# Half-row products of a recurrence, tied behind the first product of each of their two banks

## The chip, the cores and the metric

The kernel runs on one core of one Trainium2 chip, in float32. The metric is the device time of one execution in microseconds (us); lower is better. Engines by the profile's names: PE is TensorE (PEld its weight loads), DVE VectorE, ACT ScalarE, POOL GpSimd, SP SyncE, which issues the transfers.

## The reference

One layer of a hybrid block over 256 latent and 256 context tokens of width 2048. A modulated norm feeds one input projection (10,304 columns in all). Its columns go to a bidirectional RWKV-7 recurrence of 16 heads of 64 (the "time mixing"), to a latent attention of 8 heads, and to gates; the branches are merged, projected and added to the input.

What matters here is the recurrence and what prepares it:

```python
def rwkv_prepare(u_rkv, u_wd, u_ad, conv_w, w0, w_decay_up, a0, w_a_up, k_k, k_a):
    B, L, _ = u_rkv.shape
    r, k, v = jnp.split(centred_short_conv(u_rkv, conv_w), 3, axis=-1)
    wd = jnp.tanh(u_wd.reshape(B, L, 2, DECAY_LORA))
    w_log = (w0 + jnp.einsum("bldr,drc->bldc", wd, w_decay_up)).astype(f32)
    decay = jnp.exp(-jnp.exp(-jax.nn.softplus(-w_log) - 0.5))
    a = jax.nn.sigmoid((a0 + jnp.einsum("bldr,drc->bldc",
                                        u_ad.reshape(B, L, 2, AAA_LORA), w_a_up)).astype(f32))
    ...

def rwkv7_step(S, xs):
    r, w, k, v, kk, akk = xs
    sa = jnp.einsum("dbhij,dbhj->dbhi", S, -kk)
    S = S * w[..., None, :] + sa[..., :, None] * akk[..., None, :] + v[..., :, None] * k[..., None, :]
    return S, jnp.einsum("dbhij,dbhj->dbhi", S, r)
```

The two einsums with `w_decay_up` and `w_a_up` are low-rank products of rank 64, one for each of the two directions d. The scan runs over the context tokens first and then over the latent ones, forwards and backwards.

## The kernel before

The program is written for a framework that orders the instructions of each engine at compile time by priority: program order, unless a block raises its priority by a number of places. Each engine then works its own queue in that order and waits on semaphores. Tiles come from pools; a tile of a pool's tag takes one of its buffers when a former holder has been read for the last time.

The recurrence handles two heads (a pair p) at a time on 128 partitions, 64 for each, in chunks of 64 tokens. Each pair has two halves, `h // 2` = p and `h % 2` = 0 for context, 1 for latent tokens: 16 halves in all, in nine groups. `front` (line 691) prepares a half, `front2` (line 836) transposes its values and keys, `diagonal` (line 869) inverts 16x16 blocks by way of DRAM, and `back` (line 913) computes inverses of the chunks (products into PSUM tag `lv`) and steps through the chunks (tag `ch`, tiles `chp`, products with `UV`, `xs`, `M`). The function `drive` (line 545) writes the order of all this in program order, from an estimate of TensorE's time that each product adds (`Tensor.add`), and puts steps of a background between them: projections with the big weights (`proj_g`, line 410, tile `acc`) in bursts.

A burst (`Tensor.burst`, line 99) leaves its first product, the head, at its own priority, and gives all that follow in the block a priority raised by `HB` = 600 places and a dependency on the head without a semaphore (`BEHIND`), so that they come soon behind it in TensorE's queue. Before the change only the projections use it (and, later, `branch_g`).

Two places in `front` have products that read 64 of the 128 rows and write one of two banks each:

- `lr` (line 712): the low-rank products. The directions d lie on the two halves of the rows (`hss`), and direction d writes bank `lr[d]`. For each of two column halves j there are three products (high and low parts in fp32r) per direction: twelve in all, 64 rows, 256 columns. Both banks come from tag `wk`, which has two buffers. In a context half `unit_keys` (line 668) runs ahead and has its own tiles there; the last, transposes of `rnb`, is read by the instruction that makes `kk` (line 688). ScalarE reads both `lr` banks with two activations each (`th`, and the sums in `En`).
- `pv` (line 787), latent halves alone, twice each (`cp`): sixteen products of keys with queries (tiles `BK` and `QR`), 64 rows, 128 columns, head g of the pair on half g of the rows into bank `pv[g]`. VectorE masks them into `AQ` and `AR`.

Of the kernel before, what the change touches and what calls it, by code (L numbers as in the profile page):

```python
# [19 lines left out]
T = 256  # L20
# [34 lines left out]
BEHIND = mybir.DependencyInfo(mybir.DependencyClass.NoSync, mybir.DependencyReason.DATA)  # L55
# [29 lines left out]
class Tensor:  # L85
# [10 lines left out]
    head = None  # L96

    @contextmanager
    def burst(self, tc):

        self.tc, self.head = tc, ()
        yield
        self.head = None

    def matmul(self, out, lhsT, rhs, **kw):
        n, k, m = math.prod(rhs.shape[1:]), lhsT.shape[0], math.prod(lhsT.shape[1:])
        if lhsT.dtype == F32R:
            self.add((max(256, n) / 2400 + 0.003) * k / 128, n * k / 128)
        elif m <= 64:
            self.add(n / 1200 + 0.044, 2 * n * k / 128)  # L110
        else:
            self.add((max(512, 4 * n) / 2400 + 0.005) * max(k, 64) / 128, 2 * n * k / 128)
        if not self.head:
            i = self.engine.matmul(out, lhsT=lhsT, rhs=rhs, **kw)  # L114
            if self.head == ():
                self.head = i
            return i
        with self.tc.high_priority(HB):
            i = self.engine.matmul(out, lhsT=lhsT, rhs=rhs, **kw)  # L119
            self.tc.add_manual_dep(i.ins, self.head.ins.name, BEHIND, reason="burst")  # L120
        return i

    def transpose(self, *a):
# [21 lines left out]
def hybrid_block(  # L145
# [23 lines left out]
    E = Tensor(nc.tensor, clock)  # L169
# [101 lines left out]
    lrh = cvp.tile([P, 2, TT], F32R, name="lrh", bufs=1)  # L271
    lrl = cvp.tile([P, 2, TT], F32R, name="lrl", bufs=1)
    pp = ctx.enter_context(tc.tile_pool(name="pp", bufs=2, space=PSUM))
    with tc.tile_pool(name="p1", bufs=2) as p1:
# [48 lines left out]
        for k in range(KT):  # L323
# [5 lines left out]
            g = k % 4  # L329
# [261 lines left out]
    with tc.tile_pool(name="rw", bufs=1) as rw:  # L591
# [18 lines left out]
        hss = [slice(0, 64), slice(64, 128)]  # L610
# [10 lines left out]
        def wk():  # L621
            return pp.tile([P, 512], F32, name="wk", tag="wk", bufs=2)
# [68 lines left out]
        def front(h, k, mi, rho):  # L691

            p, lat = h // 2, h % 2
# [6 lines left out]
            ts = slice(t0, t0 + T)  # L700
            if not lat:
                wa = wp.tile([P, T], F32, name="th", tag="th", bufs=2)
                nc.sync.dma_start(wa, wup[p])
                wah = rw.tile([P, 2, P], F32R, name="wah")
                wal = rw.tile([P, 2, P], F32R, name="wal")
                split(wa, wah.rearrange("p j c -> p (j c)"), wal.rearrange("p j c -> p (j c)"))
                ups[p] = wah, wal
            wah, wal = ups[p]
# [1 line left out]


            lr = [wk() for _ in range(2)]
            for j in range(2):
                for x, (a, b) in enumerate(((wah, lrh), (wah, lrl), (wal, lrh))):
                    for d in range(2):
                        E.matmul(lr[d][:, T * j:T * j + T], lhsT=a[hss[d], j], rhs=b[hss[d], j, ts], start=x == 0, stop=x == 2)

            def dirs(ap):

# [38 lines left out]
            Q = rw.tile([P, 2, 4, 2, CH], F32, name="QR", bufs=2) if lat else Qbd  # L758
# [9 lines left out]
            BK = rw.tile([P, 8, 2, CH], F32, name="BK", bufs=2)  # L768
# [14 lines left out]
            if lat:  # L783
                for cp in range(2):

                    cs = slice(2 * cp, 2 * cp + 2)
                    pv = [wk().rearrange("p (d c a t) -> p d c a t", d=2, c=2, a=2) for _ in range(2)]
                    for d in range(2):
                        for c in range(2):
                            for g in range(2):  # L790
                                E.matmul(pv[g][:, d, c], lhsT=BK[hss[g], 4 * d + 2 * cp + c].rearrange("p a t -> p (a t)"),
                                         rhs=Q[hss[g], d, 2 * cp + c], start=True, stop=True)
                    for g in range(2):
                        for dst, a, m in (AQd, 0, mq), (AR, 1, mr):
                            V.tensor_tensor(dst[:, g, :, cs], pv[g][:, :, :, a], m.unsqueeze(2).to_broadcast([P, 2, 2, CH]), ALU.mult)
                    yield
            else:
                for d in range(2):
                    ps = wk()
                    pv = ps.rearrange("p (c g t) -> p c g t", c=4, g=2)  # L800
                    for c in range(4):
                        E.matmul(pv[:, c], lhsT=BK[:, 4 * d + c].rearrange("p a t -> p (a t)"), rhs=Q[:, d, c], start=True, stop=True)
                    V.tensor_tensor(AQd[:, :, d], pv.rearrange("p c g t -> p g c t"),
                                    mq[:, d].unsqueeze(1).unsqueeze(1).to_broadcast([P, 2, 4, CH]), ALU.mult)
                    yield
# [312 lines left out]
        def front_chain():  # L1118
            nonlocal keyed, fronts
            for k, hs_ in enumerate(groups):  # L1120
                rho = rw.tile([P, 2, 10], F32, name="rho", bufs=3)
                for m, h in enumerate(hs_):
                    p = h // 2
                    yield (lambda: p in cks and (h % 2 == 0 or p in crs))
                    yield from front(h, k, m, rho)
                    keyed += 1
                yield lambda: backs >= k
                UV = rw.tile([P, 2, 2, 8, CH], F32, name="UV")
                for m, h in enumerate(hs_):
                    yield lambda: h // 2 in cvs_  # L1130
                    yield from front2(h, m, UV)
                    fronts += 1
                ready[k] = UV, rho
# [317 lines left out]
    for j in range(KT):  # L1451
# [8 lines left out]
        t = mg.tile([P, T], F32, name="gt")  # L1460
# [6 lines left out]
    for cb in range(4):  # L1467
# [5 lines left out]
        for q in range(8):  # L1473
            ws = list(enumerate(weights(w_out[cb, q], 1024), 2 * q))

            for i, (k, w) in sorted(itertools.product(range(2), ws), key=(lambda x: x[0]) if q == 7 else (lambda x: x[1][0])):
                ts = slice(128 * i, 128 * i + 128)
# [127 lines left out]
```

## Time and profile before

| | before |
|---|---|
| median of 3 runs | 1291.74 us (1291.65 to 1292.87) |
| the profiled execution, time / span | 1290.54 / 1288.8 us |
| granted TensorE clock, mean | 0.991 |
| busy: PE, DVE, ACT | 1231.0, 951.4, 569.4 us |
| busy in 150 to 870 us: PE, DVE, ACT | 691.9, 585.6, 292.7 us of 720 |
| low-rank products `wk<-lrh,wah` and its like | 192, from 150.6 to 811.1 us |
| `wk<-QR,BK` | 256, from 197.7 to 838.7 us |

How to read the rows below. L114 is a line of the kernel; since all products are recorded in `Tensor.matmul`, L114 is one outside a burst or at the head of one, L119 one behind a head, L125 a transpose, and L140 all work of VectorE and ScalarE. In a row of the order of time stand the start in us, the time taken, engine, line, operation, what is written and read, "64*128" for rows and columns of TensorE in use, the shape, and xN for N like instructions merged; in square brackets the idle time ahead of the first and what ended it. In a row of a group stand the count, then busy us and mean ns, then the idle time before them. In a row of waits stand the engine and what it waited for, us in total, times, and the longest. The row of a stage has its bounds and length, busy us and count for PE, PEld, DVE, ACT and POOL, then the granted clock, the share of the DMA engines and GB/s.

### The profile page before, as it was taken

The numbers are of one execution on the slowest core, as the hardware profiler recorded it, in microseconds if no ns is written. First come the engines' busy times: TensorE is split into PE (matmuls) and PEld (weight loads), VectorE is DVE, ScalarE is ACT, GpSimd is POOL, SyncE is SP. The second block draws the span as 40 slices with busy tenths as digits, with TensorE's granted clock in tenths as the row PEclk, the third lists the DMA queues.
The fourth block names the chain that finished last, engine by engine and source line by source line (L and its number), as shares of the span: only waits on it lengthen the run. The fifth ranks groups of instructions, "written<-read, shape, count | busy, mean of one in ns | idle before, by whom it ended". The sixth has DMA issues, their size and how long they took to land.

```text
span 1288.8 us, 30049 instructions
## 1 busy us (share of the span) xinstructions
PE 1231.0 (96%) x11484; PEld 1043.3 (81%) x11484; DVE 951.4 (74%) x2658; ACT 569.4 (44%) x1183; POOL 3.3 (0%) x9
## 2 busy tenths in 40 slices
PE   5999999999999999999999988999999999999998
PEld 2666887787887788888788878988999999889887
DVE  4444776877898888879878886875787677758655
ACT  3444642442443333524434343443466555535443
POOL 0000000000000000000000000000000000000000
PEclk9999998999999999999999998999999999999999
DMA  9998444444442433433434344424665433589784
GB/s 375 349 359 317 131 153 137 138 130 113 120 132 71 120 98 105 148 109 98 125 108 136 89 134 124 120 71 146 221 205 183 123 123 103 175 269 299 224 262 140
DMA packets 172319, 212.09 MB, mean 165 GB/s; under 512 B 68560, under 2 KB 96848, under 8 KB 171664
## 3 DMA queue, kind: packets, MB, share of 16 engines
q1 hardware_dynamic: 172176, 210.18, 51.8%
q8 instruction: 90, 1.47, 0.5%
q14 instruction: 53, 0.43, 0.1%
HBM read 195.30 MB, written 14.82 MB: 163 GB/s over the span
## 4 chain that ended last, share of the span: by engine, by line
PE 70%; DMA 12%; DVE 12%; ACT 3%; issue 2%; SPq 1%; DVEq 0%; ACTq 0%
PE acc L119 26%; PE chp L114 11%; PE lv L114 9%; PE acc L114 7%; PE wk L114 6%; DMA wm<-in_w_mod_ss 4%; PE a L114 3%; PE ch L114 3%; DMA w<-in_w_proj 3%; DVE wl L140 3%; PE wk L125 2%; DVE BK L140 2%; DMA thd<-th 1%; ACT wh L140 1%; SPq L875 1%
## 5 line engine op out<-in xcount | busy, mean ns | idle before, releaser
L140 DVE TENSOR_TENSOR wl<-w,wh 128x512 fp32r<-128x512 f32 (+1 forms) x480 | 322.3, 674 | 165.0 <-ACT wh L140 88.2
L140 ACT CAST wh<-w 128x512 fp32r<-128x512 f32 (+1 forms) x484 | 290.3, 607 | 332.4 <-PE acc L119 127.8
L119 PE MATMUL acc<-hmh,wl 128*128 128x256 f32 (+1 forms) x1312 | 397.4, 303 | 3.6 <-DVE wl L140 3.2
L119 PE MATMUL acc<-hml,wh 128*128 128x256 f32 (+1 forms) x1312 | 394.0, 300 | 0.0
L119 PE MATMUL acc<-hmh,wh 128*128 128x256 f32 (+1 forms) x928 | 273.4, 295 | 0.0
L119 PEld LDWEIGHTS acc<-hmh,wl 128*128 128x128 f32 x1312 | 248.2, 189 | 19.6 <-DVE wl L140 8.5
L119 PEld LDWEIGHTS acc<-hml,wh 128*128 128x128 f32 x1312 | 248.6, 190 | 9.7 <-issue 1.0
L119 PEld LDWEIGHTS acc<-hmh,wh 128*128 128x128 f32 x928 | 175.7, 189 | 5.0
L114 PE MATMUL acc<-hmh,wh 128*128 128x256 f32 (+1 forms) x400 | 149.7, 374 | 12.6 <-ACT wh L140 7.9
L114 PEld LDWEIGHTS acc<-hmh,wh 128*128 128x128 f32 x400 | 75.6, 189 | 38.8 <-ACT wh L140 14.3
L140 DVE TENSOR_TENSOR pr<-wt 64x14 f32<-64x14 f32 (+6 forms) x224 | 42.5, 190 | 3.1
L140 DVE TENSOR_TENSOR wt<-wt,pr 64x14 f32<-64x14 f32 (+6 forms) x224 | 42.4, 189 | 3.2
L114 PE MATMUL a<-hmh,wh 128*128 128x512 f32 x96 | 41.2, 429 | 0.0
L114 PE MATMUL a<-hmh,wl 128*128 128x512 f32 x96 | 38.7, 403 | 0.4 <-DVE wl L140 0.4
L114 PE MATMUL a<-hml,wh 128*128 128x512 f32 x96 | 38.3, 399 | 0.0
L114 PE MATMUL pm<-wm,ssil 128*32 128x256 f32 x512 | 34.3, 385 | 3.7 <-DMA wm<-in_w_mod_ss 3.5
L114 PE MATMUL lv<-W,Z 64*64 64x64 f32 x1024 | 34.6, 220 | 1.9 <-DVE W L140 1.6
L140 DVE TENSOR_TENSOR W<-WT,lv 128x512 f32<-128x512 f32 x48 | 32.4, 682 | 5.5 <-PE lv L114 5.3
L114 PE MATMUL chp<-obh,wl 128*128 128x256 f32 x128 | 36.2, 283 | 0.0
L114 PE MATMUL chp<-obl,wh 128*128 128x256 f32 x128 | 36.2, 283 | 0.0
L114 PE MATMUL chp<-obh,wh 128*128 128x256 f32 x128 | 36.2, 283 | 0.0
L114 PEld LDWEIGHTS lv<-W,Z 64*64 64x64 f32 x1024 | 31.7, 135 | 5.0 <-DVE W L140 3.4
(318 smaller groups left out, 2170.8 us busy)
## 6 DMA issues: line engine op xcount, KB each, us to landing
w<-in_w_proj SPq DMA_DIRECT2D x296, 256.0 KB, 2.9
wm<-in_w_mod_ss SPq DMA_DIRECT2D x64, 512.0 KB, 7.2
w<-in_w_mod_g SPq DMA_DIRECT2D x64, 256.0 KB, 3.0
w<-in_w_br SPq DMA_DIRECT2D x64, 256.0 KB, 4.0
w<-in_w_out SPq DMA_DIRECT2D x64, 256.0 KB, 3.5
w<-in_w_first SPq DMA_DIRECT2D x32, 192.0 KB, 5.0
thd<-th SPq DMA_DIRECT2D x48, 128.0 KB, 2.8
xT<-in_xcT SPq DMA_DIRECT2D x4, 1024.0 KB, 8.7
```

Source lines behind the costliest of these rows:

```text
L114: i = self.engine.matmul(out, lhsT=lhsT, rhs=rhs, **kw)
L119: i = self.engine.matmul(out, lhsT=lhsT, rhs=rhs, **kw)
L125: return self.engine.transpose(*a)
L140: return fn(out, *a, **kw)
L875: nc.sync.dma_start(dl[:, 4 * g + b].rearrange("u r c -> r u c"), AQ[r0:r0 + 16, g, :, 16 * b:16 * b + 16])
```

## The change

A burst may have several heads: `burst(tc, heads)` leaves the first `heads` products at their own priority, and ties each of those that follow behind all of them. The twelve `lr` products and each sixteen `pv` products become such a burst with two heads, and the two halves of the rows change places in their inner loop (1 before 0), so that the heads are the first products of banks 1 and 0. Everything else, and the estimate that each product adds, stays.

```diff
     @contextmanager
-    def burst(self, tc):
-
-        self.tc, self.head = tc, ()
+    def burst(self, tc, heads=1):
+
+        self.tc, self.head, self.heads = tc, [], heads
         yield
         self.head = None
...
-        if not self.head:
-            i = self.engine.matmul(out, lhsT=lhsT, rhs=rhs, **kw)
-            if self.head == ():
-                self.head = i
-            return i
+        if self.head is None:
+            return self.engine.matmul(out, lhsT=lhsT, rhs=rhs, **kw)
+        if len(self.head) < self.heads:
+            self.head.append(self.engine.matmul(out, lhsT=lhsT, rhs=rhs, **kw))
+            return self.head[-1]
         with self.tc.high_priority(HB):
             i = self.engine.matmul(out, lhsT=lhsT, rhs=rhs, **kw)
-            self.tc.add_manual_dep(i.ins, self.head.ins.name, BEHIND, reason="burst")
+            for h in self.head:
+                self.tc.add_manual_dep(i.ins, h.ins.name, BEHIND, reason="burst")
         return i
...
             lr = [wk() for _ in range(2)]
-            for j in range(2):
-                for x, (a, b) in enumerate(((wah, lrh), (wah, lrl), (wal, lrh))):
-                    for d in range(2):
-                        E.matmul(lr[d][:, T * j:T * j + T], lhsT=a[hss[d], j], rhs=b[hss[d], j, ts], start=x == 0, stop=x == 2)
+            with E.burst(tc, 2):
+                for j in range(2):
+                    for x, (a, b) in enumerate(((wah, lrh), (wah, lrl), (wal, lrh))):
+                        for d in (1, 0):
+                            E.matmul(lr[d][:, T * j:T * j + T], lhsT=a[hss[d], j], rhs=b[hss[d], j, ts], start=x == 0, stop=x == 2)
...
                     pv = [wk().rearrange("p (d c a t) -> p d c a t", d=2, c=2, a=2) for _ in range(2)]
-                    for d in range(2):
-                        for c in range(2):
-                            for g in range(2):
-                                E.matmul(pv[g][:, d, c], lhsT=BK[hss[g], 4 * d + 2 * cp + c].rearrange("p a t -> p (a t)"),
-                                         rhs=Q[hss[g], d, 2 * cp + c], start=True, stop=True)
+                    with E.burst(tc, 2):
+                        for d in range(2):
+                            for c in range(2):
+                                for g in (1, 0):
+                                    E.matmul(pv[g][:, d, c], lhsT=BK[hss[g], 4 * d + 2 * cp + c].rearrange("p a t -> p (a t)"),
+                                             rhs=Q[hss[g], d, 2 * cp + c], start=True, stop=True)
```

## The prediction

> **What bounds the kernel now.** I read the page first, then a table of stages, then who TensorE waits for, then the order of its products around the two places that the change touches.
>
> ```profile
> span 1288.8 us, 30049 instructions
> ...
> PE 1231.0 (96%) x11484; PEld 1043.3 (81%) x11484; DVE 951.4 (74%) x2658; ACT 569.4 (44%) x1183; POOL 3.3 (0%) x9
> ...
> PE 70%; DMA 12%; DVE 12%; ACT 3%; issue 2%; SPq 1%; DVEq 0%; ACTq 0%
> ```
>
> TensorE is busy for 96% of the span and carries 70% of the chain that ended last. The products of the change all lie in the recurrence, so the next rows take its stretch alone: the table of stages, and the waits of TensorE there, longest first.
>
> ```profile
> 150.00:870.00 720.00, 691.88 (x7533) 585.46 (x7532) 585.60 (x1754) 292.73 (x632) 0.00 (x0) 0.99 0.41 117
> ...
> PE acc L114 <- ACT wh L140: 6.5, 3, 5.4
> PE wk L114 <- DVE QR L140: 4.4, 5, 1.3
> PE chp L114 <- ACT UV L140: 3.2, 4, 2.2
> ...
> PE wk L114 <- DVE BK L140: 1.6, 2, 1.3
> PE chp L114 <- DVE xs L140: 1.4, 2, 1.2
> ```
>
> In 720 us TensorE is idle for 28 (720 less 691.88), and no single releaser holds more than 6.5 of it. VectorE is busy 585.6 of 720 and ScalarE 293. Background projections (tile acc) fill whatever the recurrence leaves, and over the whole span TensorE is as full (96%). So TensorE's own time is what a change here is paid in. Busy time overlaps from one product to the next, so I count TensorE's time by the distance from one start to the next, never by durations.
>
> Two halves of a 128-row operand give two 64-row products. Here are the twelve low-rank products (line 712) of a front whose two banks were both free, in order of time.
>
> ```profile
> 451.47 0.28 PE L119 MATMUL acc<-hml,wh 128*128 128x256 f32 x1
> 451.59 0.28 PE L119 MATMUL acc<-hmh,wl 128*128 128x256 f32 x1
> 451.80 0.39 PE L114 MATMUL wk<-lrh,wah 64*128 64x256 f32 x2
> 452.02 0.28 PE L114 MATMUL wk<-lrl,wah 64*128 64x256 f32 x2
> 452.14 0.28 PE L114 MATMUL wk<-lrh,wal 64*128 64x256 f32 x2
> ...
> 452.49 0.28 PE L114 MATMUL wk<-lrh,wal 64*128 64x256 f32 x2
> 452.70 0.51 PE L114 MATMUL acc<-hmh,wh 128*128 128x512 f32 x1
> ```
>
> Each row holds two products, and the next row starts 0.12 us later, as after one 128-row product of 256 columns (451.47 to 451.59). Two products cost one slot: they run side by side. Going in (451.59 to 451.80), the first pair (451.80 to 452.02) and going out (452.49 to 452.70) take 0.21 to 0.22 instead of 0.12, so a detour from 128 rows to 64 and back costs about 0.3 us over its slots. All twelve take 0.90 us from their first start to the next product's.
>
> The same twelve in a front of the context half:
>
> ```profile
> 406.61 0.66 PE L125 MATMUL wk<-cc,rnb 128*128 128x128 f32 x4 [0.90 <-DVE rnb L140]
> 407.19 0.38 PE L114 MATMUL wk<-lrh,wah 64*128 64x256 f32 x1
> ...
> 407.88 0.28 PE L114 MATMUL wk<-lrh,wal 64*128 64x256 f32 x1
> 408.09 0.57 PE L114 MATMUL chp<-UV,AQ 128*64 128x64 f32 x12
> 408.59 0.38 PE L114 MATMUL wk<-lrh,wah 64*128 64x256 f32 x1
> ...
> 409.49 0.33 PE L114 MATMUL chp<-UV,AQ 128*64 128x64 f32 x2
> ```
>
> Six products of one bank run one by one (407.19 to 408.09, again 0.90 us), and the other six 1.4 us later (408.59 to 409.49, 0.90). Nothing is paired, and it costs 1.80 us where 0.90 would do. The cause stands in VectorE's order of time and in its group.
>
> ```profile
> 407.33 0.73 DVE L140 SCALAR_TENSOR_TENSOR kk<-ck,vv,wk 128x512 f32<-128x512 f32 x1
> ...
> L140 DVE SCALAR_TENSOR_TENSOR kk<-ck,vv,wk 128x512 f32<-128x512 f32 x8 | 5.9, 736 | 1.3 <-PE wk L125 1.3
> ```
>
> The pool wk has two banks. One holds the transposes of rnb (406.61) until kk has read them, which is at 408.06; only then is the second bank there. Going through the sixteen fronts, eight run as two sixes. The first of these sixteen sixes and the last start here, and the group of their first product follows (no idle time ahead of it).
>
> ```profile
> 150.56 0.39 PE L114 MATMUL wk<-lrh,wah 64*128 64x256 f32 x1
> ...
> 755.55 0.38 PE L114 MATMUL wk<-lrh,wah 64*128 64x256 f32 x1
> ...
> L114 PE MATMUL wk<-lrh,wah 64*128 64x256 f32 x64 | 16.1, 331 | 0.0
> ```
>
> Seven others stand in pairs already, as at 451.80, and one in pairs cut into three pieces.
>
> The products pv (line 787) of the eight latent fronts: one block whole, then the most cut and the last cut one.
>
> ```profile
> 562.11 1.16 PE L114 MATMUL wk<-QR,BK 64*128 64x128 f32 x16
> 563.21 0.68 PE L114 MATMUL chp<-xs,W 64*64 64x64 f32 x16
> ...
> 197.71 0.49 PE L114 MATMUL wk<-QR,BK 64*128 64x128 f32 x4 [0.26 <-DVE wt L140]
> 198.65 0.64 PE L114 MATMUL acc<-w,ssil 128*32 128x256 f32 x8 [0.44 <-ACT th L140]
> 199.65 0.71 PE L114 MATMUL wk<-QR,BK 64*128 64x128 f32 x6
> 200.29 0.39 PE L119 MATMUL acc<-hmh,wl 128*128 128x256 f32 x1
> ...
> 201.67 0.71 PE L114 MATMUL wk<-QR,BK 64*128 64x128 f32 x6
> 202.31 0.39 PE L114 MATMUL acc<-hmh,wh 128*128 128x256 f32 x1
> ...
> 723.10 0.90 PE L114 MATMUL wk<-QR,BK 64*128 64x128 f32 x10 [1.21 <-DVE QR L140]
> 723.93 1.14 PE L114 MATMUL lv<-WT,AQ 64*64 64x64 f32 x30
> 725.00 0.71 PE L114 MATMUL wk<-QR,BK 64*128 64x128 f32 x6
> 725.64 0.62 PE L114 MATMUL acc<-w,ssil 128*32 128x256 f32 x2
> ```
>
> There are 16 blocks of 16. They run in 26 pieces, so ten pieces are extra.
>
> **The change part by part.** No product, load, copy or transfer is added or removed; the ties are an order made at compile time, not an instruction, so they cost nothing themselves (a higher count than 30049 would show otherwise). No queue of transfers is moved past.
>
> *Low-rank products.* Only the head of the free bank can now run early; the other eleven come once the second bank is there. A lone head is a detour with one slot, 0.3 plus 0.12 less the step that any product has (0.12), so about 0.31 us. Eleven products make five pairs and one single, six slots, whichever head came first: 0.90. Together 1.21 against 1.80, 0.59 per front, five slots of 0.118. Eight fronts: 4.7 us. The seven paired fronts had both banks at their first product and stay as they are: 0. The front in three pieces I leave out; its gain would come on top.
>
> *pv.* A whole block takes 1.10 us (562.11 to 563.21). The one cut in two takes 0.83 and 0.64 (723.10 to 723.93, 725.00 to 725.64), 0.37 more. The one cut in three takes 0.64, 0.64 and 0.50 (197.71 to 198.65 less the 0.44 of idle), 0.68 more for two cuts. So 0.34 a cut, and ten cuts: 3.4 us. All sixteen read Q, which VectorE finishes last (the wait on QR), so the tie to the heads adds no wait for operands.
>
> *What is queued behind.* ScalarE reads both low-rank banks, two activations of 128x256 for each, of which this is the group of one kind:
>
> ```profile
> L140 ACT ACTIVATE En<-wk,dv 128x256 f32<-128x256 f32 x32 | 14.7, 469 | 0.0
> ```
>
> Until now the first bank's two, 0.94 us at 469 ns each, ran while the second bank was still coming; now all four follow the burst. The front can be up to 0.94 us later in eight fronts. The low end is 0, as the burst also ends earlier; the high end is 8 times 0.94, 7.5 us. What says how often TensorE stands waiting for such a front is the wait on BK, two times in the whole stage, so I take two fronts: 1.9 us.
>
> *Priority.* The rest of each burst now passes other products by up to 600 places. What it passes, products of the back chain (chp, lv) above all, is done later by at most one block, 0.90 or 1.10 us, while TensorE's total stays. The rows nearest are the waits on UV and xs, 3.2 and 1.4: between a gain of these 4.6 and a loss of as much. I take 0, because in the front shown the back chain's sixteen products (408.09 and 409.49) are cut by the second six, and a lone head lets them run together earlier, which weighs against the delays elsewhere.
>
> *The reversed order of the halves.* A pair takes a slot whichever half stands first: 0.
>
> Sum: 4.7 + 3.4 - 1.9 = 6.2 us. The profiled execution took 1290.54 us (span 1288.8), the runs' median 1291.74, 1.2 above it. So 1284.3 profiled, and a median of 1285.5.
>
> A rule that speaks against the change: the Trainium skill, "TensorEngine Tiling (Array Packing)", Key Properties, says that changing the tiling mode drains TensorE, and a lone head is a mode of its own. The trace agrees that there is a price (0.21 against 0.12). Were each drain a product's whole 0.28 rather than 0.10, eight lone heads would cost 8 times 0.36 more, 2.9, and the median would be 1288.4.
>
> **The rivals.** *The heads come together.* If the scheduler has other work and both heads fall into one run, a front costs 0.90 instead of 1.80 and no detour is left: 7.2 + 3.4 = 10.6, and ScalarE loses little: 1281.1. For it: the second six start 0.5 us after kk has ended, so the banks are less than a run apart. Against: the first six were placed at once because that bank was free, and a lone head is ready there too.
>
> *The gain is hidden.* The front chain sets the pace, and ScalarE's shift counts in all eight fronts: 8.1 (4.7 + 3.4) - 7.5 = 0.6, a median of 1291.1, no change to be measured. For it: TensorE does wait for QR (4.4 us, five times) at pv. Against: 28 us of idle in 720 leave little to a chain.
>
> *Slower: TensorE stands at the second head.* If the scheduler puts the second head, with its ten followers, close behind the first, it waits in TensorE's queue for kk, and all that is behind it waits too. The first six covered that wait with 0.90 us; a lone head covers 0.31 (407.19 to 407.50, against kk's end at 408.06). That is 0.56 us, and 1.3 more where VectorE runs as late as the longest waits on QR and BK show: 1.9 per front, 14.9 in eight, less 8.1: 6.8 slower, 1298.5. It decides from 1.0 us per front (8.1 over 8). Against: in that front twelve products stood between the two sixes, so there is work to put there. That products are never reordered past a waiting one is also what the Trainium skill says, "TensorE: Matmul & The Clock Gate", Part 3 (strict FIFO); the wait at 723.10, with 1.21 us of idle ahead, agrees.
>
> **How the numbers follow.** I give the forecast 0.50, the heads together 0.17, the gain hidden 0.19, the wait at the second head 0.14. Within 0.2%, 2.6 us, is about what a measurement of this kernel can't tell from no change. Faster is the first two, 0.67; the same 0.19; slower 0.14. The forecast's own range is 1283 to 1289, its terms' bounds without the extremes of ScalarE's shift. The range from 1279 to 1294 holds the forecast, the hidden gain, and the heads together up to 2 us beyond their sum; it leaves out the wait at the second head and a little below, less than 2 in 10.
>
> **What would show it.** Rows of the low-rank products should be x2 in all fronts, with one x1 ahead and one at the end in eight of them, and pv in 16 pieces of 16 (18 with lone heads). The idle of TensorE ahead of wk<-lrh,wah, 0 now, must stay near 0; several us there is the slow rival. Waits on QR and BK above 6.0 us together show the hidden gain. If the blocks stand whole, these waits have not grown, and the time still has not moved, then the count of slots is wrong: TensorE's time was not what the recurrence is paid in.

## The result, and the profile after

The changed kernel takes 1283.63 us (median of 6 runs, 1280.1 to 1287.46), the kernel before 1292.94 beside it (6 runs, 1291.65 to 1295.05): a ratio of 0.9931, 95% interval 0.9907 to 0.9955. It is faster by 0.69%, 9.3 us between the medians; 6.2 were forecast. The page of its profiled execution (1282.83 us):

```profile
span 1281.0 us, 30018 instructions
...
PE 1223.5 (96%) x11484; PEld 1035.8 (81%) x11484; DVE 953.4 (74%) x2658; ACT 567.2 (44%) x1183; POOL 3.3 (0%) x9
```

The same number of products and of everything else; 31 instructions fewer in all. The front of the context half that the prediction showed, in order of time on TensorE (lines have moved: L116 is a head, L119 what follows it, L126 a transpose):

```profile
402.33 0.66 PE L126 MATMUL wk<-cc,rnb 128*128 128x128 f32 x4 [0.47 <-DVE rnb L141]
402.91 0.38 PE L116 MATMUL wk<-lrh,wah 64*128 64x256 f32 x1
403.22 0.68 PE L114 MATMUL chp<-UV,AQ 128*64 128x64 f32 x14
...
405.42 0.38 PE L116 MATMUL wk<-lrh,wah 64*128 64x256 f32 x1
405.43 0.50 PE L119 MATMUL wk<-lrl,wah 64*128 64x256 f32 x2
405.65 0.39 PE L119 MATMUL wk<-lrh,wal 64*128 64x256 f32 x2
...
406.00 0.39 PE L119 MATMUL wk<-lrh,wal 64*128 64x256 f32 x2
406.32 0.68 PE L114 MATMUL chp<-xs,W 64*64 64x64 f32 x16
```

A lone head takes 0.31 us (402.91 to 403.22), the eleven others 0.90 (405.42 to 406.32), 0.11 to 0.12 for two. In this front fourteen of the back chain's products now run straight behind the head. Eight fronts have this form, the first at 152.23 and the last at 742.61; the front that stood in three pieces is one block.

The pv products stand in 19 pieces instead of 26. One correction to the text above: a pv block is eight products, each of which the profile records twice; "sixteen" there counts records. The block at the former 723 us is whole, and one of the two that are still cut is the second pv block of its front:

```profile
293.64 0.49 PE L116 MATMUL wk<-QR,BK 64*128 64x128 f32 x2
295.16 0.37 PE L116 MATMUL wk<-QR,BK 64*128 64x128 f32 x1
...
713.49 0.49 PE L116 MATMUL wk<-QR,BK 64*128 64x128 f32 x4
713.81 0.84 PE L119 MATMUL wk<-QR,BK 64*128 64x128 f32 x12
714.58 1.14 PE L114 MATMUL lv<-WT,AQ 64*64 64x64 f32 x30
```

The stage of the recurrence and TensorE's waits in it, as above:

```profile
150.00:870.00 720.00, 691.99 (x7679) 585.08 (x7679) 593.33 (x1767) 293.70 (x637) 0.00 (x0) 0.99 0.42 120
...
PE acc L116 <- ACT wh L141: 6.3, 2, 5.3
PE chp L114 <- ACT UV L141: 4.2, 8, 2.3
PE acc L119 <- DVE wl L141: 3.5, 6, 1.2
PE wk L116 <- DVE QR L141: 2.7, 3, 2.0
...
PE wk L114 <- DVE BK L141: 1.6, 2, 1.4
```

In the same 720 us TensorE is as busy and does 146 records more (7679 against 7533). The waits on QR and BK have shrunk from 6.0 to 4.3 us.

To see where the time went I added up, for each TensorE product from the first kk on, the distance to the next product's start, less the idle time between them, by what it writes. In us:

| kernel (profiled execution) | low-rank | pv | lv | idle | first kk to end |
|---|---|---|---|---|---|
| before | 22.0 | 20.9 | 158.7 | 35.9 | 1138.1 |
| changed | 16.8 | 18.6 | 156.5 | 34.7 | 1128.7 |
| changed, again (e9) | 16.7 | 18.6 | 156.4 | 35.4 | 1129.7 |
| e6, no ties | 24.2 | 31.8 | 157.8 | 29.5 | 1147.1 |
| e10, fixed order, pairs broken | 21.1 | 26.4 | 156.3 | 31.5 | 1140.0 |
| e11, fixed order, blocks joined | 16.9 | 18.7 | 157.2 | 49.6 | 1147.2 |
| e12, fixed order, no lone head | 14.8 | 18.6 | 156.4 | 35.4 | 1127.3 |

The blocks themselves save 5.2 and 2.3 us, the inverse's products between them (lv), which now stand in 86 runs instead of 99, 2.2 more, and idle time 1.2. All other products together take 1.4 us longer (897.0 against 895.6), so 9.4 are left in the last column.

### The profile page after: what moved, and what is told of

Its sections match the earlier page's. It is cut to its first block, busy times and chain, and to the rows that moved or that the text cites. A ratio compares the mean times of both kernels' runs of the same rounds, so it can differ in the third digit from the quotient of the medians.

```text
span 1281.0 us, 30018 instructions
## 1 busy us (share of the span) xinstructions
PE 1223.5 (96%) x11484; PEld 1035.8 (81%) x11484; DVE 953.4 (74%) x2658; ACT 567.2 (44%) x1183; POOL 3.3 (0%) x9
## 4 chain that ended last, share of the span: by engine, by line
PE 66%; DVE 14%; DMA 13%; issue 2%; ACT 2%; SPq 2%; DVEq 0%; ACTq 0%
PE acc L119 25%; PE chp L114 10%; PE lv L114 10%; DMA wm<-in_w_mod_ss 5%; PE acc L116 4%; DMA w<-in_w_proj 4%; PE a L114 3%; DVE wl L141 3%; PE ch L114 3%; PE wk L114 3%; PE wk L126 2%; DVE BK L141 2%; PE acc L114 2%; DVE wt L141 1%; PE wk L119 1%
## 5 line engine op out<-in xcount | busy, mean ns | idle before, releaser
L119 PE MATMUL acc<-hmh,wl 128*128 128x256 f32 (+1 forms) x1312 | 397.7, 303 | 4.3 <-DVE wl L141 4.0
L119 PE MATMUL acc<-hml,wh 128*128 128x256 f32 (+1 forms) x1312 | 394.8, 301 | 0.0
L119 PE MATMUL acc<-hmh,wh 128*128 128x256 f32 (+1 forms) x928 | 274.0, 295 | 0.0
L119 PEld LDWEIGHTS acc<-hmh,wl 128*128 128x128 f32 x1312 | 249.0, 190 | 20.0 <-DVE wl L141 8.0
L119 PEld LDWEIGHTS acc<-hml,wh 128*128 128x128 f32 x1312 | 249.7, 190 | 9.3 <-issue 1.0
L119 PEld LDWEIGHTS acc<-hmh,wh 128*128 128x128 f32 x928 | 176.4, 190 | 4.9
L116 PE MATMUL acc<-hmh,wh 128*128 128x256 f32 (+1 forms) x384 | 145.1, 378 | 11.7 <-ACT wh L141 7.0
L116 PEld LDWEIGHTS acc<-hmh,wh 128*128 128x128 f32 x384 | 72.9, 190 | 36.8 <-ACT wh L141 13.1
L141 ACT COPY UV<-chp 64x256 f32<-64x256 f32 (+1 forms) x36 | 12.2, 339 | 59.3 <-PE chp L114 59.0
```

The lines of the kernel that those rows point to most:

```text
L116: self.head.append(self.engine.matmul(out, lhsT=lhsT, rhs=rhs, **kw))
L141: return fn(out, *a, **kw)
```

## The experiments

All ratios are to the kernel before, measured beside it.

| run | ratio | 95% interval |
|---|---|---|
| e1, low-rank products alone | 0.9928 | 0.9900 to 0.9956 |
| e2, pv alone | 0.9963 | 0.9943 to 0.9984 |
| e3, the changed kernel's queue again | 0.9905 | 0.9869 to 0.9941 |
| e4, heads together in most fronts | 0.9886 | 0.9848 to 0.9925 |
| e5, products of a bank in a row, free order | 0.9924 | 0.9898 to 0.9950 |
| e6, priority without ties | 1.0043 | 1.0023 to 1.0064 |
| e7, ties without priority | 0.9946 | 0.9927 to 0.9966 |
| e8, half 0 before half 1 | 0.9903 | 0.9875 to 0.9931 |
| e9, the changed kernel again | 0.9915 | 0.9885 to 0.9944 |
| e10, fixed order, pairs broken | 0.9970 | 0.9947 to 0.9993 |
| e11, fixed order, blocks joined | 1.0025 | 1.0008 to 1.0043 |
| e12, fixed order, no lone head | 0.9890 | 0.9864 to 0.9915 |

### One part at a time (e1, e2)

e1 takes `with E.burst(tc, 2)` off pv and restores its loop, e2 does so for the low-rank products:

```diff
-                    with E.burst(tc, 2):
-                        for d in range(2):
-                            for c in range(2):
-                                for g in (1, 0):
+                    for d in range(2):
+                        for c in range(2):
+                            for g in range(2):
```

> The changed kernel with the sixteen pv products as before, so only the low-rank products are tied. Theory A (TensorE's slots, one for one): eight fronts save five slots of 0.118 us, 4.7, and the front that stood in three pieces saves 0.6: 5.3 us faster than before, ratio 0.996. Theory B (placement: the gain is that the recurrence's own steps are cut less, pairs are worth nothing): nothing to derive from slots; the changed kernel's whole 9.3 or none of it. Theory C (any new order moves the time by some us either way): a ratio that does not add up with that of pv alone to the changed kernel's 0.993.

> The changed kernel with the twelve low-rank products as before, so only pv is tied. Theory A: seven of the ten cuts go, 0.34 us each: 2.4 us faster than before, ratio 0.998. Theory B: nothing from slots; if pv's place is what counts, most of 9.3. Theory C: does not add up with the low-rank part alone.

Measured: 0.72% and 0.37% faster. Both parts help. The low-rank part gives more than its slots (0.41%, just outside its interval); for pv the slots (0.19%) lie inside the interval. Their sum, 1.09%, stands beside 0.69 to 0.95% for the changed kernel's three measurements (this one, e3 and e9), so the parts add up within the intervals. Theory C, chance, is not needed for them.

### Pairs against place (e3, e5)

e3 wrote the products of the block one half after the other:

```diff
+                low_rank(1, 0, 0)
+                low_rank(0, 0, 0)
+                for d in (1, 0):
+                    for j in range(2):
+                        for x in range(3):
+                            if j or x:
+                                low_rank(d, j, x)
```

> The changed kernel with the same two heads, ties and place of the low-rank block, but behind the heads all products of one half of the rows come before those of the other, so that they can't run in pairs. Theory A: eight fronts with a lone head lose five slots of 0.118 us again and the eight others six, 88 slots, 10.4 us: slower than the changed kernel by 10.4, ratio to before about 1.001. Theory B: the place is kept, so the time stays with the changed kernel's, ratio 0.993.

It tells nothing of pairs: the order at compile time put the products back into pairs, and TensorE's queue came out product for product as the changed kernel's. So 0.9905 is a second measurement of the changed kernel. e5 ties each product behind the one before it, so that the queue really has a bank's products in a row:

```diff
+                last = None
+                for d, j, x in [(1, 0, 0)] + [(0, j, x) for j in range(2) for x in range(3)] + [(1, j, x) for j in range(2) for x in range(3)][1:]:
...
+                    if last:
+                        tc.add_manual_dep(i.ins, last.ins.name, BEHIND, reason="burst")
+                    last = i
```

and the like for pv.

> The changed kernel with its heads, ties and the place of every block kept, and inside each block the products tied one behind the other, all of half 0 before the rest of half 1, so that at most the heads and one more pair run side by side. Theory A (TensorE's slots, one for one): each of sixteen low-rank blocks takes ten slots of 0.118 us instead of six, 7.6 us, and each of sixteen pv blocks thirteen of 0.112 instead of eight, 9.0 us: 16.6 us slower than the changed kernel, ratio to before about 1.004. Theory B (placement; pairs are worth nothing): as the changed kernel, 0.992.

Measured 0.9924, as theory B has it and not A (1.004). In its trace the blocks do take 8.8 us more than the changed kernel's (20.4 and 23.8 against 16.8 and 18.6), but idle time is 4.7 less (30.0), which leaves 4.1. The raw ratio hides this: e5's runs had a mean granted clock of 0.9916, the kernel before beside them 0.9885. Brought to one clock, as in the last section, e5 is 3.9 us slower than the changed kernel, which is what its trace says, and not theory B. It isn't a clean test in any case: with the blocks longer, about a quarter of TensorE's queue had been ordered anew. That is why the last three runs fix every queue.

### Ties and priority apart (e6, e7)

```diff
-            for h in self.head:
+            for h in self.head if self.heads == 1 else ():
```

```diff
-        with self.tc.high_priority(HB):
+        with self.tc.high_priority(HB if self.heads == 1 else 0):
```

> The changed kernel with the raised priority behind the heads but without the ties, so that the products of a bank follow their own head alone and no block runs in pairs. Theory A: against before, eight more low-rank fronts lose five slots of 0.118 us, 4.7, less 0.6 for the front in three pieces, and sixteen pv blocks seven slots of 0.112, 12.5: 16.6 us slower than before, ratio 1.013. Theory B (priority and place do it): faster than before, like the changed kernel, 0.992.

> The changed kernel with the ties but without the raised priority behind the two heads. The low-rank blocks stay whole but for one, which is cut in three; pv is cut as before the change. Theory A: 4.7 us faster than before from the low-rank slots and nothing from pv, ratio 0.996; the raised priority is then worth the cuts of pv alone. Theory B (the priority moves the recurrence's steps forward): the gain goes, 1.000.

Without ties (e6) every block stands in the queue one bank after the other and the kernel is 0.43% (5.6 us) slower than before. Theory B falls here, but A expected 1.3%: the blocks grew by 13.1 us (24.2 and 31.8 against 22.0 and 20.9), and 6.4 us of idle went, which leaves 6.7. Without priority (e7) most of the low-rank gain stays (17.4 us in the blocks) and pv is cut as before (21.0): 0.54% faster, at A's 0.996 within the interval. So the tie makes the pairs. What the raised priority is worth the ratios don't separate from nothing; brought to one clock, e7 is 3.5 us slower than the changed kernel, and its blocks take 3.0 us more, mostly the cuts of pv.

### Which half stands first (e8)

```diff
-                        for d in (1, 0):
+                        for d in range(2):
```

and the same for g in pv.

> The changed kernel with half 0 before half 1 again, in both places. Theory A: a pair takes a slot whichever half stands first, so the time of the changed kernel, ratio 0.992. Theory C (any new order moves the time by some us): off from that by more than the intervals.

0.9903: the changed kernel's time. The order of the halves does nothing that these runs can tell.

### The heads together (e4, e12)

In e4 the first head of a context half is also ordered behind the instruction that makes kk (kept as `made[p]`):

```diff
+                            i = E.matmul(lr[d][:, T * j:T * j + T], ...)
+                            if not lat and j + x == 0:
+                                tc.add_manual_dep(i.ins, made[p].ins.name, BEHIND, reason="burst")
```

> The changed kernel, with the first low-rank head of a context half also ordered (at compile time) behind the instruction that makes kk and frees the second bank, so that both heads come in one run in five more of the eight fronts. Theory A: five detours of 0.31 us less, 1.6 us faster than the changed kernel, ratio to before about 0.992. The slow rival of the prediction (TensorE stands at the second head): with no lone head to cover it, up to 0.56 us of idle for each of the five fronts, 2.8 us, so 1.2 slower than the changed kernel, 0.994; idle time then stands ahead of the rows of the low-rank products.

0.9886, the fastest ratio of all, though not separated from the changed kernel's; idle ahead of the low-rank products is 0.1 us in all. e12 does the same with nothing else free to move: the order of all four queues is taken from the changed kernel, written into the program as one chain each, and only the eight lone heads moved into their blocks.

```diff
+    for steps in ORDER.values():
+        last = None
+        for n in itertools.accumulate(map(int, steps.split())):
+            i = nc.find_inst_by_name(f"I-{n}")
+            if last is not None:
+                tc.add_manual_dep(i, last, BEHIND, reason="order")
+            last = f"I-{n}"
```

The numbers in `ORDER` name the instructions of each queue, and the burst's own priority and tie are left out for the two kinds of blocks, since the chain holds their order.

> The changed kernel with the order of every queue fixed, and only the eight lone low-rank heads moved behind, into their block, so that all sixteen blocks are whole. Theory A: eight detours of 0.31 us less, 2.5 us faster than the changed kernel, ratio 0.989. The slow rival (a wait at the second head without cover): TensorE comes 0.3 us earlier to the block, so up to 0.3 us of idle in eight places eats the gain: as the changed kernel, 0.991, with idle time ahead of the rows of the low-rank products.

The table of numbers moves the lines of these kernels: L355 is a product of a block or outside a burst, L360 one behind a projection's head, L366 and L367 a transpose, L381 and L382 VectorE and ScalarE. Here the same front, and the group of the blocks' first products with their idle time (0.1) at the end of its row:

```profile
399.98 0.66 PE L367 MATMUL wk<-cc,rnb 128*128 128x128 f32 x4 [0.47 <-DVE rnb L382]
400.56 0.68 PE L355 MATMUL chp<-UV,AQ 128*64 128x64 f32 x14
...
402.76 0.39 PE L355 MATMUL wk<-lrh,wah 64*128 64x256 f32 x2
...
L355 PE MATMUL wk<-lrh,wah 64*128 64x256 f32 x64 | 11.1, 329 | 0.1
```

The back chain's products follow the transposes at once, the block waits for nothing, and its time falls by 1.9 us (14.8 against 16.7). The kernel beside it on that chip is e9: 0.9890 against 0.9915, 0.25% or 3 us, in the direction and of the size of eight detours (2.5), but the intervals overlap. The slow rival isn't seen: no wait takes the head's place.

### The order fixed: what a slot is worth (e9, e10)

e10 has e12's chains with the changed kernel's own order; only inside the blocks, the products of one bank stand before those of the other.

> The changed kernel once more, as the base for the next three on the same chip. All theories: ratio 0.991, as in the runs so far (0.993 and, for two kernels whose TensorE order is the same or nearly so, 0.990).

> The changed kernel with the order of every queue (TensorE, VectorE, ScalarE, SyncE) written down and fixed, and only inside the blocks the products of one bank put before those of the other, so that no more than one pair a block runs side by side and nothing else has moved. Theory A (TensorE's slots, one for one): eight low-rank blocks five slots of 0.118 us more, eight with a lone head four, 8.5; sixteen pv blocks seven of 0.112, 12.5: 21 us slower than the changed kernel, ratio to before 1.007. Theory D (added slots partly fill time in which TensorE waits anyway, as the serial run with a free order had it, 4 of 9 us): 9 to 10 us slower, ratio 0.998 to 0.999. Theory B (pairs are worth nothing, the place is): 0.991.

e10 is at 0.9970 and e9 at 0.9915. With nothing moved, breaking the pairs costs 0.55%, about 7 us (4 to 10 by the spread of the runs). Theory B falls, and so does A's 21. Two things made it smaller. First, the blocks grew by 12.2 us and not by 21 (21.1 and 26.4 against 16.7 and 18.6); the section on hardware says why. Second, of these 12.2 us 3.9 came out of idle time (31.5 against 35.4): TensorE arrived later at places where it would have waited. That leaves 8.3, and the times brought to one clock give 7.3 to 9.3, by which measurement of the changed kernel is taken. (The last column of the table differs by 10.3, because the unchanged products took 2.1 longer in that execution, at a granted clock of 0.989 against 0.990.) So about two thirds of a slot reaches the end, theory D's form with a size at or a little below its 9 to 10.

### The order fixed: the blocks joined in the kernel before (e11)

Chains as in e12, with the order of the kernel before, and only the blocks' products moved together.

> The kernel before with the order of every queue written down and fixed, and only the products of the blocks moved together: in eight fronts one low-rank head stays, the other five go behind the second bank's first product in pairs, the front in three pieces and eight cuts of pv are joined. Nothing else moves. Theory A: 4.7 + 0.6 + 2.7 = 8.0 us faster than before, ratio 0.994, and what the changed kernel has beyond that, 2 to 3 us, is its other new order. Theory B (the gain is the order of the rest): 1.000. If ScalarE's shift (up to 7.5 us) counts, it shows here most, since ScalarE's own order can't adapt: 0.995 to 1.000.

It is slower than before, 1.0025. The blocks take what the changed kernel's take (16.9 and 18.7), 7.3 us less than before, yet idle time grows from 35.9 to 49.6. The stage, TensorE's waits with ScalarE in the first two rows, then what ScalarE's activations wait for, and one front in order of time on ScalarE and TensorE:

```profile
150.00:870.00 720.00, 679.82 (x7460) 573.13 (x7459) 579.24 (x1733) 287.22 (x622) 0.00 (x0) 0.99 0.42 117
...
PE acc L355 <- ACT wh L381: 9.4, 8, 6.5
PE chp L355 <- ACT UV L381: 6.5, 10, 2.2
...
ACT th L381 <- PE wk L355: 27.6, 14, 4.1
...
498.71 0.47 ACT L381 ACTIVATE th<-wk,dv 128x256 f32<-128x256 f32 x1 [2.98 <-PE wk L355]
499.08 0.47 ACT L381 ACTIVATE En<-wk,dv 128x256 f32<-128x256 f32 x1
499.44 0.36 ACT L381 COPY UV<-chp 64x256 f32<-64x256 f32 x1
...
499.84 0.33 PE L355 MATMUL chp<-AR,UV 128*64 128x64 f32 x2 [0.81 <-ACT UV L381]
```

and in the kernel before (with its th at the same place) and in the changed one, the same waits of ScalarE:

```profile
ACT th L140 <- PE wk L114: 20.6, 20, 2.3
...
496.23 0.47 ACT L140 ACTIVATE th<-wk,dv 128x256 f32<-128x256 f32 x1 [1.74 <-PE wk L114]
...
ACT th L141 <- PE wk L119: 5.3, 9, 1.1
ACT th L141 <- PE wk L114: 2.4, 2, 1.5
...
406.32 0.84 ACT L141 ACTIVATE th<-wk,dv 128x256 f32<-128x256 f32 x2 [0.94 <-PE wk L119]
407.05 0.84 ACT L141 ACTIVATE En<-wk,dv 128x256 f32<-128x256 f32 x2
```

In e11 ScalarE's queue still has the first bank's th at its old place. It stands there for 2.98 us (1.74 in the kernel before), the copy of UV that the back chain needs stands behind it, and TensorE waits 0.81 us for that copy. This comes three times, at 499.84, 586.64 and 673.46; in the kernel before TensorE has no such wait at these three places. In the changed kernel the queue was ordered anew: the two th come side by side, behind the burst, and their wait is 5.3 us, against 18.2 before and 25.2 in e11 (each sum above without the 2.4 us of another th). By TensorE's releasers, from the first kk to the end, e11 waits 7.7 us more for ScalarE than the kernel before (20.3 against 12.6) and 6.3 more for VectorE (27.7 against 21.4), whose order was kept too. How much of the latter follows from ScalarE isn't shown, and the old order, fixed with nothing joined, was not run. So the tie alone, in a program whose other queues stay, is a loss; the gain needs the other engines' order to follow.

## Why the prediction was right

The measured gain, 9.3 us, is one and a half times the 6.2 forecast, inside the range. By its own steps:

- *Low-rank products, 4.7 us.* Right as a mechanism, place and size: eight lone heads of 0.31 us, eleven products in 0.90, the seven other latent fronts whole. The trace gives 5.2 with the front in three pieces, which was left out.
- *pv, 3.4 us.* Right in kind, too large: seven of the ten cuts went, 2.3 us.
- *The free reversal of halves: 0.* e8 agrees.
- *Priority: 0.* e7 sets it at about the price of pv's cuts (3.5 us at one clock), which the pv term holds already.
- *ScalarE's shift, 1.9 us lost.* This step failed. I costed it as if ScalarE's order were kept, and the compile-time order took it away: the waits on QR and BK fell from 6.0 to 4.3 us, and TensorE's waits for ScalarE (wh and UV in the stage) stayed about the same, 9.7 and 10.5 us. In its place stands a gain: the inverse's products are cut less, 2.2 us in lv. The danger was real: in e11, with ScalarE's order kept, TensorE waits 7.7 us more for ScalarE, about the 7.5 of the upper bound, and as much as 13.7 us more in all.
- *"TensorE's own time is what a change here is paid in", one for one.* Too simple. e10 shows about two thirds reaching the end. By that share the blocks' 7.5 us are worth some 5 of the 9.3 (an estimate); the rest came with the new order of the other work, which the sum had at a loss of 1.9. That the sum came as near as it did is luck in that part: a share too high on one side and a gain left out on the other. What in that new order makes the rest isn't settled. e11, where no other order followed, has nothing of the gain, and ScalarE's queue is the one place where its trace shows how.

A lone head costs what the rows showed: removing eight took 1.9 us out of the blocks and 1.2 out of what precedes them (the other products into wk, 77.8 us against 79.0) in e12, 0.39 each, near the 0.31 and not at the 0.67 (0.31 and 0.36) of the dearer drain in the prediction. The Trainium skill's rule that a change of tiling mode drains TensorE ("TensorEngine Tiling (Array Packing)", Key Properties) gives no price; the one here is that of the rows.

Of the rivals, *the heads together* is a further step (e4, e12) and not what the change does. *The gain is hidden* did not come, nor did *TensorE stands at the second head*: idle ahead of the low-rank rows stayed at 0, and also with no lone head (0.1 in e12).

## What to carry to other kernels

Look in order of time whether products that could share the array come out as x2 or as two runs; here the bank that a VectorE read still held (kk) had split them, and a tie behind the first product of each bank mended it. When a burst is held back on one engine, ask what stands behind its readers in the other queues: the same joined blocks are 0.7 to 0.95% faster where all queues are ordered anew, and 0.25% slower where every other queue keeps its order, ScalarE's early reader in front included. And price saved slots of a 96% busy engine below one for one (here at about two thirds), since part of them only turns into waiting.

## What the hardware showed unexpectedly

TensorE starts products of the other half of the rows ahead of older ones in its queue. In e10 the queue has the low-rank block in this order (six of bank 0, then five of bank 1, by what they read):

```
lrh,wah  lrl,wah  lrh,wal  lrh,wah  lrl,wah  lrh,wal | lrl,wah  lrh,wal  lrh,wah  lrl,wah  lrh,wal
```

and the trace, in order of time:

```profile
155.67 0.38 PE L355 MATMUL wk<-lrh,wah 64*128 64x256 f32 x1
155.89 0.28 PE L355 MATMUL wk<-lrl,wah 64*128 64x256 f32 x1
156.01 0.28 PE L355 MATMUL wk<-lrh,wal 64*128 64x256 f32 x1
156.02 0.38 PE L355 MATMUL wk<-lrl,wah 64*128 64x256 f32 x1
156.13 0.28 PE L355 MATMUL wk<-lrh,wah 64*128 64x256 f32 x1
156.24 0.28 PE L355 MATMUL wk<-lrh,wal 64*128 64x256 f32 x1
156.25 0.28 PE L355 MATMUL wk<-lrl,wah 64*128 64x256 f32 x1
156.36 0.28 PE L355 MATMUL wk<-lrh,wah 64*128 64x256 f32 x1
156.36 0.28 PE L355 MATMUL wk<-lrh,wal 64*128 64x256 f32 x1
156.47 0.28 PE L355 MATMUL wk<-lrl,wah 64*128 64x256 f32 x1
156.59 0.28 PE L355 MATMUL wk<-lrh,wal 64*128 64x256 f32 x1
```

The fourth to start is a lrl,wah, which is the seventh in the queue (the fourth is a lrh,wah): bank 1's first product runs beside bank 0's third, ahead of three older ones. Three pairs form in this way, and eleven products take 1.13 us (155.67 to the next product at 156.80). With the ten slots that I had counted it would be about 1.37 (0.90 and four of 0.118). The eight blocks of eleven all stand in this order and take 1.13 us (0.90 in pairs), the eight of twelve take 1.22 to 1.25. The strict order that the prediction cited ("TensorE: Matmul & The Clock Gate", Part 3, of the Trainium skill) does not hold between the two halves of the rows; for a product that waits on a semaphore, as at 723.10 above, no run here shows anything passing it.

The granted clock differs from run to run of one kernel, between 0.982 and 0.993 in the kernel before, and the time with it: a line through all 187 runs that have a clock on record, fitted within kernels, gives 1.12 us for each 0.001. That alone is up to 12 us between two runs, more than the change. Brought to a clock of 0.990 by that line, the kernel before is at 1294.5 us (standard error 0.3), the changed kernel at 1283.4, 1284.5 and 1285.4 in its three measurements (0.4 to 0.8; 1284.4 together), e5 at 1288.3 (0.8), e7 at 1287.9 (0.5), e10 at 1292.7 (0.5), e11 at 1298.7 (0.4) and e12 at 1282.6 (0.6). Whether a kernel's own work moves its clock, so that the line takes out a part of its effect, these runs don't show.
